# Tile sizes that shift where SBUF tiles lie, in a one-core hybrid encoder step

## The chip, the cores and the metric

The kernel runs on one core of one Trainium2 chip. The metric is device time of one execution in microseconds (us). Before the change the median of three runs is 1943.49 us (1939.63 to 1945.09).

## The reference, cut to what matters

One layer of a streaming encoder: 2048 prompt frames and 64 frames of a running stream, model width 1024. A combined input projection feeds three groups (a gated recurrence "HGRN2" with 8 heads, retention with 4 heads, cross-attention to 256 memory tokens with 4 heads); each group's output is multiplied by a SiLU gate, all three are concatenated to 2048 columns and go through one output projection, a residual and a final norm.

```python
def mixer_layer(x, pos, s_hg, s_rt, mem_k, mem_v, norm_g, w_in, lb, hg_norm_g, rt_norm_g, w_out):
    h = rms_norm(x, norm_g)
    proj = h @ w_in
    hg_q, hg_f, hg_i, hg_gate, rt_q, rt_k, rt_v, rt_gate, xa_q, xa_gate = jnp.split(proj, _split_points(), axis=-1)
    ...
    mixed = jnp.concatenate([o_hg, o_rt, o_xa], axis=-1)
    out = x + mixed @ w_out
    return out, s_hg_new, s_rt_new
```

All inputs and outputs are float32.

## The kernel before, in words

**Split products.** TensorE multiplies in a reduced form of float32 (`float32r`, F32R in the code). So that the products keep their accuracy, `split` (lines 239 to 241) turns every operand of a large product into a high part, which ScalarE rounds (line 240), and a low part, which VectorE gets as the difference (line 241). Each product is then three matmuls into the same accumulator: high with high, high with low, low with high. In `T.matmul(out, a, b)` the operand `a` is stationary (loaded into the array by LDWEIGHTS) and `b` is moving (streamed past it).

**Stages.** A short start makes the memory keys and values. Then two groups of tokens (0 to 1023, and 1024 to 2111 with the sample frames at the end) go through the input projections and the three head groups. Last comes the output stage from line 1192 on, one tile of 128 tokens after another, 16 of them and one of the 64 sample frames.

**The large products.**
- Line 249, in `gemm_col`: weights stationary, normed activations moving, 24 matmuls for each column tile of 128 outputs and up to 512 tokens. Tiles: `whi`, `wlo` from the pool `wpool`; `ha`, `hb` from `hpool`.
- Line 294, in `gemm_tok`: the same two families of tiles with their roles exchanged, activations stationary, 512 columns of weights moving.
- Lines 741 and 785, in the attention's tail: both operands are tiles `s` of the pool `wk`, which hold a split of queries, keys, values and softmax weights.
- Line 1180, in `y_half`: the output projection. Stationary are the split mixed activations `m`, tiles `s` of the pool `wk` that line 1042 takes and line 1048 fills; moving are the split output weights, which stand in `whi`/`wlo`, in the former places of `ha` and `hb`, and in two pairs of tiles `v` of `vpool` (the list `worder`, line 847). A half tile is 16 blocks of the contraction with three matmuls each, 48 in all; two halves make a token tile. For the 64 sample frames each half is 32 matmuls.

The smaller products are plain float32 and show up in the trace as two MATMUL records each: lines 516 to 581 for HGRN2 (line 563 with stationary `abuf`, line 566 with stationary `s` and moving state `Sn` or `Sc`), 620 to 693 for retention (moving `q2b` in line 637 and `r2` in line 653), 763 for attention.

**Order.** TensorE's and SyncE's order is that in which the code is written: `poll` (line 107) lets the tails of heads in between the large products when a modelled clock has passed their due times. The other engines are ordered by a scheduler. Tiles come from pools with a fixed number of buffers; `small` (line 223) takes little tiles for sums and scales from the pool `sm`, two buffers for those of 32 columns and three for the others. A tile that gets a buffer again waits for the readers of the buffer's former tile.

**Addresses.** Pools lie one behind the other in each SBUF partition, in the order of lines 74 to 87 (`const`, `wk`, `sm`, `vpool`, `qep`, `stt_p`, `hpool`, `wpool`, `stp`), and tiles inside a pool likewise, each rounded up to 32 bytes. Sizes of the large tiles, and the steps at which the matmuls cut them, are multiples of 256 bytes, so that everything in such a pool has one remainder modulo 256.

Of the kernel before, what the change touches and what calls it, by code (L numbers as in the profile page):

```python
# [7 lines left out]
F32 = mybir.dt.float32  # L8
# [7 lines left out]
P = 128  # L16
# [47 lines left out]
def layer_kernel(ctx: ExitStack, tc: tile.TileContext, io: dict):  # L64
    nc = tc.nc
    V, S, G, T = nc.vector, nc.scalar, nc.gpsimd, nc.tensor
    dma = nc.sync.dma_start
# [6 lines left out]
    const = ctx.enter_context(tc.tile_pool(name="const", bufs=1))  # L74
    wk = ctx.enter_context(tc.tile_pool(name="wk", bufs=16))
    sm = ctx.enter_context(tc.tile_pool(name="sm", bufs=3))
# [114 lines left out]
        wpos["credit"] += 1  # L191
        w_pump()

    cols = const.tile([P, 44], F32, name="cols")
    dma(cols, io["cols"])
    cst = const.tile([P, 396], F32, name="cst")
    ident = cst[:, 0:128]
    qdec = cst[:, 128:384].rearrange("p (a b) -> p a b", a=2)
# [2 lines left out]
    mask = const.tile([P, 512], U8, name="mask")  # L201
    ones = const.tile([P, P], F32, name="ones")
    G.memset(ones, 1.0)
    nhalf = const.tile([P, 4], F32, name="nhalf")
    G.memset(nhalf, -0.5)
    a_buf = []
    for i in range(2):
# [13 lines left out]
        return wk.tile([P, 512], dt, tag="s", name="s")  # L221

    def small(n, tag):
        return sm.tile([P, n], F32, tag=tag, name=tag, bufs=2 if n == 32 else 3)

    def acc():
        return p_acc.tile([P, 512], F32, tag="acc", name="acc")
# [77 lines left out]
    def stats_g(chunks, c0, gap):  # L305
        for i, src in enumerate(chunks):
            L = src.shape[0]
            ss = small(2, "ss2")
            for j in range(2):
                x = slot()  # L310
                dma(x[0:L], src[:, j * 512:(j + 1) * 512])
                S.activation(x[0:L], x[0:L], AF.Square, accum_out=ss[0:L, j:j + 1])
            rs = rsall[0:L, c0 + i:c0 + i + 1]
            G.tensor_tensor(out=rs, in0=ss[0:L, 0:1], in1=ss[0:L, 1:2], op=ALU.add)
            rsqrt_small(rs, rs, 1, 1.0 / D, EPS)
            rsdone.add(c0 + i)
            yield gap
# [113 lines left out]
    def hgrn_gemm(h, wf, wq, wg, ht, tok0, nt, vt, rel):  # L431
# [22 lines left out]
        for w in (1, 2, 4, 8):  # L454
# [3 lines left out]
            v4 = Gt[:, 0:ntp].rearrange("p (n t w) -> p n t w", t=2, w=w)  # L458
            V.tensor_tensor(out=v4[:, :, 0, :], in0=v4[:, :, 0, :], in1=bc(v4[:, :, 1, 0:1], [P, n, w]), op=ALU.mult)
        Te = small(32, "Te")[:, 0:nb].rearrange("p (c a) -> p c a", a=8)  # L460
        V.tensor_copy(Te, F[:, 0:ntp].rearrange("p (c a w) -> p c a w", a=8, w=SUB)[:, :, :, SUB - 1])
        rT = small(32, "rT")[:, 0:nb].rearrange("p (c a) -> p c a", a=8)
        V.reciprocal(out=rT, in_=Te)
        M = sm.tile([P, 4, 36], F32, tag="M", name="M", bufs=2)[:, 0:nch, :]
# [353 lines left out]
        hmap[gi, i] = ht  # L818
        hdone[gi, i] = done

    rsall = const.tile([P, 20], F32, name="rsall")
    t0 = const.tile([P, 8], F32, name="t0")
    V.tensor_tensor(out=t0, in0=cols[:, 0:8], in1=cols[:, 8:16], op=ALU.subtract)
    S.activation(t0, t0, AF.Tanh, scale=0.5)
    ca = const.tile([P, 8], F32, name="ca")
    cb = const.tile([P, 8], F32, name="cb")
    cnb = const.tile([P, 8], F32, name="cnb")
    hgg = const.tile([P, 12], F32, name="hgg")
    V.tensor_scalar(out=ca, in0=t0, scalar1=0.25, scalar2=0.75, op0=ALU.mult, op1=ALU.add)
    V.tensor_scalar(out=cb, in0=t0, scalar1=-0.25, scalar2=0.25, op0=ALU.mult, op1=ALU.add)  # L830
    V.tensor_scalar(out=cnb, in0=t0, scalar1=0.25, scalar2=-0.25, op0=ALU.mult, op1=ALU.add)
# [475 lines left out]
```

## Time and profile before

| | |
|---|---|
| median of 3 runs | 1943.49 us |
| the profiled execution | 1944.17 us, of which the trace's span is 1942.4 us |
| TensorE (PE) matmul busy | 1908.9 us, 98% |
| VectorE (DVE), ScalarE (ACT), GpSimd (POOL) busy | 54%, 30%, 7% |
| granted TensorE clock | 0.995 of full speed on average |
| memory read and written | 117.69 and 33.69 MB |

In a view by line, a row has line, engine, operation, output tile, input tiles (buffer numbers left out; of a MATMUL the moving one stands first), shape, count, busy time and mean duration. A view of one tile gives minimum, median and maximum duration in ns. A matmul's duration contains its way through the array, so that following matmuls overlap; how fast they follow is read from their starts, or from the chain of waits, where a piece gives start, length and the number of instructions in it.

### The profile page before, as it was taken

The numbers are of one execution on the slowest core, as the hardware profiler recorded it, in microseconds if no ns is written. First come the engines' busy times: TensorE is split into PE (matmuls) and PEld (weight loads), VectorE is DVE, ScalarE is ACT, GpSimd is POOL, SyncE is SP. The second block draws the span as 40 slices with busy tenths as digits, with TensorE's granted clock in tenths as the row PEclk, the third lists the DMA queues.
The fourth block names the chain that finished last, engine by engine and source line by source line (L and its number), as shares of the span: only waits on it lengthen the run. The fifth ranks groups of instructions, "written<-read, shape, count | busy, mean of one in ns | idle before, by whom it ended". The sixth has DMA issues, their size and how long they took to land.

```text
span 1942.4 us, 28116 instructions
## 1 busy us (share of the span) xinstructions
PE 1908.9 (98%) x10938; PEld 1618.5 (83%) x10938; DVE 1043.3 (54%) x2512; ACT 585.9 (30%) x1414; POOL 139.9 (7%) x335
## 2 busy tenths in 40 slices
PE   8999999999999999999999999999999999999998
PEld 7888788888888787988789998899989878888886
DVE  8527457753677557417637774477765642222222
ACT  7413232322333434312323332233333431111111
POOL 0001000000100100000101111021100000000000
PEclk9999999999999999999999999999999999999999
DMA  7512222111111424212211111111122342233322
GB/s 254 179 58 55 75 66 61 44 50 44 44 55 55 153 71 134 92 55 58 87 47 49 49 49 49 44 49 49 60 71 78 118 144 87 87 102 113 89 71 60
DMA packets 116742, 153.21 MB, mean 79 GB/s; under 512 B 13312, under 2 KB 79232, under 8 KB 116608
## 3 DMA queue, kind: packets, MB, share of 16 engines
q1 hardware_dynamic: 116608, 151.41, 25.4%
q8 instruction: 86, 1.41, 0.3%
q14 instruction: 48, 0.39, 0.1%
HBM read 117.69 MB, written 33.69 MB: 78 GB/s over the span
## 4 chain that ended last, share of the span: by engine, by line
PE 87%; DVE 6%; DMA 2%; ACT 2%; issue 1%; POOL 1%; SPq 0%; DVEq 0%; POOLq 0%; ACTq 0%
PE acc L249 39%; PE acc L1180 19%; PE acc L294 15%; PE scb L522 2%; PE ob L531 2%; PE ob L563 1%; PE ob L566 1%; PE acc L785 1%; PE ob L741 1%; PE acc L264 1%; PE tr L516 1%; PE tr L581 1%; PE tr L763 1%; DVE wlo L241 1%; ACT s L682 1%
## 5 line engine op out<-in xcount | busy, mean ns | idle before, releaser
L249 PE MATMUL acc<-hb,whi 128*128 128x320 f32 (+2 forms) x1696 | 409.1, 331 | 0.4 <-DVE hb L371 0.4
L249 PE MATMUL acc<-ha,whi 128*128 128x512 f32 x1120 | 354.7, 398 | 0.0
L249 PEld LDWEIGHTS acc<-hb,whi 128*128 128x128 f32 x1696 | 284.6, 189 | 25.0 <-issue 4.4
L241 DVE TENSOR_TENSOR wlo<-wst,whi 128x1024 fp32r<-128x1024 f32 x115 | 140.0, 1226 | 261.2 <-ACT whi L240 260.2
L249 PE MATMUL acc<-hb,wlo 128*128 128x256 f32 (+2 forms) x848 | 276.9, 327 | 0.0
L249 PEld LDWEIGHTS acc<-ha,whi 128*128 128x128 f32 x1120 | 205.0, 189 | 41.3 <-issue 2.6
L249 PE MATMUL acc<-ha,wlo 128*128 128x512 f32 x560 | 220.0, 393 | 0.0
L240 ACT CAST whi<-wst 128x1024 fp32r<-128x1024 f32 x115 | 119.7, 1051 | 211.4 <-PE acc L249 172.0
L249 PEld LDWEIGHTS acc<-hb,wlo 128*128 128x128 f32 x848 | 160.2, 189 | 11.2
L294 PE MATMUL acc<-whi,ha 128*128 128x512 f32 x512 | 161.0, 396 | 0.0
L294 PE MATMUL acc<-whi,hb 128*128 128x512 f32 x512 | 160.0, 394 | 0.0
L1180 PE MATMUL acc<-whi,s 128*128 128x512 f32 x396 | 125.9, 396 | 1.3 <-ACT s L240 1.0
L249 PEld LDWEIGHTS acc<-ha,wlo 128*128 128x128 f32 x560 | 105.7, 189 | 23.1 <-DVE wlo L241 0.2
L294 PEld LDWEIGHTS acc<-whi,hb 128*128 128x128 f32 x512 | 94.5, 188 | 19.8 <-issue 1.2
L294 PEld LDWEIGHTS acc<-whi,ha 128*128 128x128 f32 x512 | 93.8, 188 | 19.6 <-issue 1.3
L294 PE MATMUL acc<-wlo,ha 128*128 128x512 f32 x256 | 100.1, 391 | 0.0
L294 PE MATMUL acc<-wlo,hb 128*128 128x512 f32 x256 | 99.8, 390 | 0.0
L1180 PE MATMUL acc<-hb,s 128*128 128x512 f32 x400 | 97.7, 400 | 0.0
L1180 PE MATMUL acc<-ha,s 128*128 128x512 f32 x400 | 96.3, 396 | 0.0
L1180 PEld LDWEIGHTS acc<-hb,s 128*128 128x128 f32 x400 | 76.3, 191 | 18.4
L241 DVE TENSOR_TENSOR s<-mst,s 128x512 fp32r<-128x512 f32 (+1 forms) x64 | 40.4, 671 | 94.2 <-ACT s L240 94.2
L1180 PEld LDWEIGHTS acc<-whi,s 128*128 128x128 f32 x396 | 74.3, 188 | 19.6 <-ACT s L240 1.3
(236 smaller groups left out, 2913.3 us busy)
## 6 DMA issues: line engine op xcount, KB each, us to landing
wst<-w_in_t SPq DMA_DIRECT2D x104, 512.0 KB, 4.0
mixT<-s SPq DMA_DIRECT2D x64, 256.0 KB, 4.3
mst<-mixT SPq DMA_DIRECT2D x30, 512.0 KB, 5.9
wst<-w_out_t SPq DMA_DIRECT2D x16, 512.0 KB, 4.0
xq<-x_prompt SPq DMA_DIRECT2D x18, 256.0 KB, 5.0
o_yp<-xq SPq DMA_DIRECT2D x18, 256.0 KB, 2.3
s<-mixT SPq DMA_DIRECT2D x16, 256.0 KB, 3.0
s<-x_prompt SPq DMA_DIRECT2D x16, 256.0 KB, 5.3
```

The lines of the kernel that those rows point to most:

```text
L240: S.copy(hi, src)
L241: V.tensor_tensor(out=lo, in0=src, in1=hi.bitcast(F32), op=ALU.subtract)
L249: T.matmul(ps[:, 0:nt], w[a][:, kk, :], ht[b][:, kk, 0:nt], start=(n == 0), stop=(n == 23))
L264: T.matmul(ps[:, 0:nt], w[a][:, kk, :], ht[b][:, kk, 0:nt], start=(kk == 0 and a + b == 0), stop=(kk == KT - 1 and a == 1))
L294: T.matmul(ps[0:L, :], ht[b][:, kk, o:o + L], w[a][:, kk % 2, :], start=(n == 0), stop=(n == 23))
L516: T.transpose(trk[:, c * 128:(c + 1) * 128], kch[:, c * 128:(c + 1) * 128], ident)
L522: T.matmul(scb[32 * e:32 * e + 32, c * 128 + 32 * e:(c + 1) * 128], K[:, c * 128 + 32 * e:c * 128 + 32 * e + 32], Qe[:, c, E_OFF[e]:E_OFF[ ...
L531: T.matmul(db[:, c * 128:(c + 1) * 128], kT[:, c * 128:(c + 1) * 128], vt[c], start=True, stop=True)
L563: T.matmul(ob[:, c * 128:(c + 1) * 128], A[:, c * 128:(c + 1) * 128], vt[c], start=True, stop=first)
L566: T.matmul(ob[:, c * 128:(c + 1) * 128], qst[:, c * 128:(c + 1) * 128], st[c][0], start=False, stop=True)
L581: T.transpose(tro[:, c * 128:(c + 1) * 128], on[:, c * 128:(c + 1) * 128], ident)
L1180: T.matmul(ps, m[a][:, kk % 4], w[b], start=(n == 0), stop=(n == 16 * len(terms) - 1))
```

## The change

No instruction is added, removed or moved on any engine: apart from names and line numbers each engine's row of instructions is the same (`nhalf` is set over 16 columns instead of 4). What differs is sizes:

```diff
-    cols = const.tile([P, 44], F32, name="cols")
-    dma(cols, io["cols"])
+    cols = const.tile([P, 60], F32, name="cols")
+    dma(cols[:, 0:44], io["cols"])
...
-    nhalf = const.tile([P, 4], F32, name="nhalf")
+    nhalf = const.tile([P, 16], F32, name="nhalf")
...
     def small(n, tag):
-        return sm.tile([P, n], F32, tag=tag, name=tag, bufs=2 if n == 32 else 3)
+        return sm.tile([P, n], F32, tag=tag, name=tag, bufs=2 if n == 32 or tag in ("rs1", "mu", "rc", "rs4", "nm", "sum", "ss2") else 3)
...
-    rsall = const.tile([P, 20], F32, name="rsall")
+    rsall = const.tile([P, 64], F32, name="rsall")
+    hgg = rsall[:, 20:32]
...
-    hgg = const.tile([P, 12], F32, name="hgg")
```

The tile `hgg` (halved gains of the heads) becomes a part of `rsall` (the tokens' norm factors, columns 0 to 18). Seven kinds of little tiles have two buffers instead of three. From this the tiles' addresses follow, as the two programs place them, as remainders modulo 256 bytes:

| tiles | before | after |
|---|---|---|
| `s` (`wk`): stationary in line 1180, both operands in 741 and 785 | 192 | 128 |
| `v` (`vpool`), `Qe`, `Sn`/`Sc`, `ha`/`hb`, `whi`/`wlo`, the staging tiles | 160 | 128 |
| `abuf`, `r2`, `q2b`, `sp` (`const`) | 160 | 0 |
| `cst` with the identity | 64 | 128 |
| `ones` | 128 | 192 |

So in lines 249 and 294 both operands have one remainder before and after, in lines 741 and 785 too; in line 1180 the stationary operand's was 192 and the moving one's 160, and now both are 128. In line 563 both were 160, and now they are 0 and 128; in lines 637 and 653 they were 160 and 192, and now 0 and 128.

## The prediction

> **What bounds the kernel now.** I read the page first, then the chain of waits in order of time, then the tiles of the large products.
>
> ```profile
> span 1942.4 us, 28116 instructions
> ...
> PE 1908.9 (98%) x10938; PEld 1618.5 (83%) x10938; DVE 1043.3 (54%) x2512; ACT 585.9 (30%) x1414; POOL 139.9 (7%) x335
> ...
> PEclk9999999999999999999999999999999999999999
> ...
> PE 87%; DVE 6%; DMA 2%; ACT 2%; issue 1%; POOL 1%; SPq 0%; DVEq 0%; POOLq 0%; ACTq 0%
> PE acc L249 39%; PE acc L1180 19%; PE acc L294 15%; PE scb L522 2%; PE ob L531 2%; PE ob L563 1%; PE ob L566 1%; PE acc L785 1%; PE ob L741 1%; PE acc L264 1%; PE tr L516 1%; PE tr L581 1%; PE tr L763 1%; DVE wlo L241 1%; ACT s L682 1%
> ```
>
> TensorE is busy for 98% of the span and carries 87% of the chain, at a clock that stays in the highest digit throughout. So the kernel's time is a number of matmuls multiplied by the distance at which one follows the other. An edit that only moves tiles can act here through that distance. The chain in order of time gives it (start, length, what, count):
>
> ```profile
> 83.75 55.76 PE acc L294 x246
> ...
> 253.03 19.73 PE acc L249 x87
> 306.11 6.85 PE acc L249 x30
> 327.11 7.53 PE acc L249 x33
> ...
> 1572.85 362.34 PE acc L1180 x1546
> ```
>
> In the long pieces the 512-column matmul costs 55.76 / 246 = 226.7 ns in line 294 and 19.73 / 87 = 226.8 ns in line 249. In line 1180 it is 362.34 / 1546 = 234.4 ns. That last number contains the waits of the output stage's first tile, so I take the cadence of whole token tiles from VectorE, which adds the residual right behind each half (the timeline of VectorE; `xq` and `abuf` alternate by tile):
>
> ```profile
> 1708.39 1.29 DVE L241 TENSOR_TENSOR s<-mst,s 128x512 fp32r<-128x512 f32 x2 [0.51 <-ACT s L240]
> ...
> 1718.68 0.69 DVE L1189 TENSOR_TENSOR xq<-xq,acc 128x512 f32<-128x512 f32 x1 [8.39 <-PE acc L1180]
> ...
> 1741.08 0.69 DVE L1189 TENSOR_TENSOR abuf<-abuf,acc 128x512 f32<-128x512 f32 x1 [8.32 <-PE acc L1180]
> ```
>
> From 1718.68 to 1741.08 us are 22.40 us for one tile of 96 matmuls: 233.3 ns each, 6.5 ns more than the same shape costs in lines 249 and 294. The views of lines 294 and 1180 show the same difference with one and the same moving tile:
>
> ```profile
> L294 PE MATMUL acc<-whi,ha x512: 387/389/504, 83.6 to 1207.9; 128*128 128x512 f32 x171
> ...
> L1180 PE MATMUL acc<-whi,s x396: 392/396/500, 1552.0 to 1931.7; 128*128 128x512 f32 x198
> ```
>
> The moving `whi` (named first) goes past a stationary `ha` in line 294 and the matmul takes 389 ns; in line 1180 it goes past a stationary `s` and it takes 396 ns (minimum, median, maximum; these durations overlap). The shape, the moving tile and the order of the three terms are the same in both lines; the stationary tile is not. Line 1180 pairs a stationary `s` at remainder 192 modulo 256 with a moving tile at 160. Line 294 pairs 160 with 160. Is it that 192 is a bad place for a stationary tile? The attention's second product has both operands at 192:
>
> ```profile
> L785 PE MATMUL acc<-s x144: 192/387/397, 662.6 to 1572.5; 128*128 128x512 f32 x72, 128*128 128x256 f32 x48, 128*128 128x64 f32 x24
> ```
>
> Its median, which falls to the 512-column matmuls (half of all, and the longest), is 387 ns. So what goes with the slow matmuls is the difference between the two operands' remainders, not either remainder.
>
> **The change part by part.** *Line 1180: 192 against 160 becomes 128 against 128.* I take it that the matmul then costs what it costs with equal remainders elsewhere. For the chain's last piece that is 1546 x (233.3 - 226.8 ns) = 10.0 us. It lies wholly on the path: the piece runs to 7 us before the end, and nothing else is on it. What is late next? The following tile's operands would be the candidate. Their last split (line 241, 1708.39 + 1.29 = 1709.68 us) is done 9.0 us before the matmuls that need it, which begin about when the tile before ends (1718.68 us). A tile gets shorter by 96 x 6.5 ns = 0.6 us, so this cover holds.
>
> *Lines 249 and 294: equal remainders, 160 before, 128 after.* I take 0. Two places with equal remainders, 160 and 192, cost the same within 2 ns in the medians above, so a third one should. There is something to gain here, though. Shorter pieces, which start behind the tail of a head, cost more per matmul:
>
> ```profile
> 145.51 2.77 PE acc L294 x12
> ...
> 321.86 4.82 PE acc L249 x21
> ```
>
> They are 2.77 - 12 x 0.2268 = 0.05 us and 4.82 - 21 x 0.2268 = 0.06 us above the long pieces' rate; the 30 and 33 above are 0.05 us over as well. Each seems to pay once for its start. If part of that is the switch between tiles of different remainders, some of it goes. With 40 HGRN2 tails and 20 of attention (8 and 4 heads on 5 token tiles) and 17 of retention, at three or four stages each, there are some 240 such starts, worth 12 us in all. I take 0 and let half of it, 6 us, set the range's lower end.
>
> *The plain float32 products with `const` tiles: lines 563, 637 and 653 now pair 128 with 0.* The timeline of TensorE in the HGRN2 tail, and the groups by shape:
>
> ```profile
> 1163.86 0.39 PE L563 MATMUL ob<-v,abuf 128*128 128x128 f32 x2
> 1164.08 0.39 PE L566 MATMUL ob<-Sc,s 128*128 128x128 f32 x2
> 1164.30 0.39 PE L563 MATMUL ob<-v,abuf 128*128 128x128 f32 x2
> 1164.53 0.39 PE L566 MATMUL ob<-Sn,s 128*128 128x128 f32 x2
> ```
>
> ```profile
> L563 PE MATMUL ob<-v,abuf 128*128 128x128 f32 x272 | 51.1, 274 | 0.0
> ...
> L653 PE MATMUL ob<-r,s 128*128 128x256 f32 x60 | 17.9, 380 | 0.0
> L637 PE MATMUL scb<-q2b,s 128*128 128x256 f32 x64 | 17.7, 401 | 2.9 <-ACT s L628 2.8
> ```
>
> Line 563 has both operands at 160, line 566 has 160 and 192, and each takes 0.22 us per pair of records. These products do not care about a difference of 32. The nearest price for a difference of 128, should they care about that, is line 1180's: (272 + 60 + 64) x 6.5 ns = 2.6 us. The other end is a like gain, since lines 637 and 653 differ by 32 already: 124 x 6.5 ns = 0.8 us. I take 0, by the row nearest to it.
>
> *Two buffers instead of three for seven kinds of little tiles.* A writer now waits for the reader two uses back instead of three. In the view of TensorE's waits stands what hangs on them today:
>
> ```profile
> PE ob L741 <- DVE s L574: 4.3, 2, 2.2
> ...
> PE tr L693 <- DVE s L685: 1.4, 2, 0.8
> ```
>
> Lines 574 and 685 read `rs`; TensorE waits for them 5.7 us in all. What would queue behind such a wait is GpSimd's next pair of lines 236 and 237 and then VectorE's line 574. The readers of two tails back are several hundred matmuls in the past, so I take 0; the upper bound is that these waits double, 5.7 us. A gain is excluded, because a buffer less can release nothing earlier. `nhalf`, `cols` and `hgg` inside `rsall` cost 0: they are written at the start, and `hgg` is read in columns that nobody writes later.
>
> The sum is -10.0 us. Against the profiled execution, 1944.17 - 10.0 = 1934.2 us. The median of the runs shown is 0.7 us below that execution, so the time should be 1943.49 - 10.0 = 1933.5 us.
>
> **The rivals.** *The address has nothing to do with it.* Line 1180 could be slower for another reason that goes with the output stage: 48 matmuls into one accumulator instead of 24, or stores and loads beside it. Then nothing changes: 1943.5 us. For it speaks that no matmul of the output stage has equal remainders, so the trace has no counterexample inside the stage. Against it speaks that line 1180 is slow on every one of its moving tiles while the other engines do less there than in the projections. The Trainium skill (SBUF — State Buffer, section "Who interferes with whom") gives TensorE two separate read ports in SBUF, one for the moving operand and one for LDWEIGHTS, and says that "PE and ACT never wait on anyone". By that rule no placement could matter and the result would be this one; the 389 against 396 ns with one moving tile disagree with it as far as a trace of one kernel can. I give it 15%.
>
> *Half of it.* The difference modulo 256 may be one condition of several, such as which part of the memory the two tiles lie in. If line 1180 settles halfway, at 230 ns, the gain is 1546 x 3.3 ns = 5.1 us: 1938.4 us, 0.26% and so within what can be told. 7%.
>
> *Slower: 128 is a bad shared place.* Both good pairs of the trace lie at odd multiples of 32 or 64 (160 and 192). None lies at 128. If tiles at 128 get in each other's way as 192 and 160 do, line 1180 gains nothing and the projections pay:
>
> ```profile
> L249 PE MATMUL acc<-ha,whi 128*128 128x512 f32 x1120 | 354.7, 398 | 0.0
> L249 PE MATMUL acc<-ha,wlo 128*128 128x512 f32 x560 | 220.0, 393 | 0.0
> L249 PE MATMUL acc<-hb,whi 128*128 128x512 f32 x544 | 171.8, 397 | 0.0
> L294 PE MATMUL acc<-whi,ha 128*128 128x512 f32 x512 | 161.0, 396 | 0.0
> L294 PE MATMUL acc<-whi,hb 128*128 128x512 f32 x512 | 160.0, 394 | 0.0
> ...
> L249 PE MATMUL acc<-hb,wlo 128*128 128x512 f32 x272 | 106.5, 391 | 0.0
> L294 PE MATMUL acc<-wlo,ha 128*128 128x512 f32 x256 | 100.1, 391 | 0.0
> L294 PE MATMUL acc<-wlo,hb 128*128 128x512 f32 x256 | 99.8, 390 | 0.0
> ```
>
> These are 4032 matmuls of 512 columns; at 6.5 ns each they cost 26.2 us, which makes 1969.7 us. It decides the sign once they lose 10.0 us / 4032 = 2.5 ns each while line 1180 still gains. Against it speaks that 160 and 192, two different places, cost the same. 8%.
>
> **How the numbers follow.** The forecast has 70%, the rivals 15, 7 and 8. What a measurement of this kernel can tell from no change is about 0.3%, 5.8 us. Faster by more than that is the forecast alone; within it are the first two rivals, 22%; slower is the last, 8%. The forecast's own bounds are 1933.5 - 0.8 - 6 = 1926.7 and, with 2.6 us of float32 products and 5.7 us of waits, 1941.8 us. To reach eight in ten, the range must take in part of the other cases: 1927.0 to 1943.5 us holds the forecast's cases, the half and half of the case without change, and leaves out some 16%.
>
> **What the changed profile would show.** If each step is right: a token tile in the output stage takes 96 x 226.8 ns = 21.8 us instead of 22.4, the last piece of the chain has about 226.8 ns per matmul, and the median of line 1180's MATMUL rows falls from 396 to about 389 ns. Line 249's and 294's long pieces stay at 226.7 to 226.8 ns, line 563's pairs at 0.22 us, and TensorE's waits behind lines 574 and 685 at about 6 us. The prediction is wrong if line 1180 stays at 233 ns, or if it falls and lines 249 and 294 give it back.

## The result, and the profile after

The changed kernel takes 1930.89 us (median of 6 runs, 1929.27 to 1935.75); the kernel before, with the runs made beside it, 1941.96 us (6 runs, 1939.63 to 1947.36). The ratio is 0.9943 with a 95% interval of 0.9924 to 0.9963: 0.4 to 0.8% faster, about 11 us. The forecast was 1933.5 us, in a range of 1927.0 to 1943.5.

The profiled execution's span went from 1942.4 to 1932.0 us, 10.4 us less. Its page and its chain of waits in order of time:

```profile
span 1932.0 us, 28118 instructions
...
PE 1899.2 (98%) x10938; PEld 1620.5 (84%) x10938; DVE 1043.5 (54%) x2512; ACT 585.9 (30%) x1414; POOL 141.3 (7%) x335
```

```profile
83.77 55.77 PE acc L294 x246
...
252.96 19.72 PE acc L249 x87
306.01 6.85 PE acc L249 x30
326.96 7.53 PE acc L249 x33
...
1572.06 352.75 PE acc L1180 x1546
```

TensorE is busy for 9.7 us less with the same number of matmuls. The page counts two instructions more than before: they are one semaphore instruction each on ScalarE and on GpSimd, so the rows of those two engines are not quite the same, though the section on the change says so. The kernel of run b below has both of them too and takes as long as the kernel before. The projections' pieces shown are the same to 0.01 us, and the output stage's begins 0.8 us earlier and is 9.6 us shorter. VectorE's residual additions show the cadence of its token tiles, and the view of lines 1180 and 294 the matmuls' durations (minimum, median, maximum):

```profile
1704.34 1.29 DVE L241 TENSOR_TENSOR s<-mst,s 128x512 fp32r<-128x512 f32 x2 [0.39 <-ACT s L240]
...
1714.48 0.69 DVE L1189 TENSOR_TENSOR xq<-xq,acc 128x512 f32<-128x512 f32 x1 [8.26 <-PE acc L1180]
...
1736.24 0.69 DVE L1189 TENSOR_TENSOR abuf<-abuf,acc 128x512 f32<-128x512 f32 x1 [7.55 <-PE acc L1180]
```

```profile
L1180 PE MATMUL acc<-whi,s x396: 388/389/500, 1549.9 to 1921.5; 128*128 128x512 f32 x198
```

```profile
L294 PE MATMUL acc<-whi,ha x512: 387/390/502, 83.6 to 1205.5; 128*128 128x512 f32 x171
```

A tile takes 21.76 us, 226.7 ns for each of its 96 matmuls, where it took 22.40 us. Line 1180's matmul now lasts what line 294's does. The float32 pairs and TensorE's waits behind the little tiles:

```profile
1161.41 0.38 PE L563 MATMUL ob<-v,abuf 128*128 128x128 f32 x2
1161.62 0.39 PE L566 MATMUL ob<-Sc,s 128*128 128x128 f32 x2
1161.85 0.39 PE L563 MATMUL ob<-v,abuf 128*128 128x128 f32 x2
```

```profile
PE ob L741 <- DVE s L574: 4.1, 2, 2.1
...
PE tr L693 <- DVE s L685: 1.4, 2, 0.8
```

Both are as before: 0.22 us a pair and 5.5 us of waits (5.7 before).

### The profile page after: what moved, and what is told of

Read it like the earlier page. It is cut to its first block, busy times and chain, and to the rows that moved or that the text cites. A ratio compares the mean times of both kernels' runs of the same rounds, so it can differ in the third digit from the quotient of the medians.

```text
span 1932.0 us, 28118 instructions
## 1 busy us (share of the span) xinstructions
PE 1899.2 (98%) x10938; PEld 1620.5 (84%) x10938; DVE 1043.5 (54%) x2512; ACT 585.9 (30%) x1414; POOL 141.3 (7%) x335
## 4 chain that ended last, share of the span: by engine, by line
PE 88%; DVE 6%; ACT 2%; DMA 2%; issue 1%; POOL 1%; SPq 0%; DVEq 0%; POOLq 0%; ACTq 0%
PE acc L249 39%; PE acc L1180 18%; PE acc L294 16%; PE scb L522 2%; PE ob L531 2%; PE ob L563 1%; PE ob L566 1%; PE acc L785 1%; PE ob L741 1%; PE acc L264 1%; ACT s L682 1%; PE tr L516 1%; PE tr L763 1%; PE tr L581 1%; POOL rs L237 1%
## 5 line engine op out<-in xcount | busy, mean ns | idle before, releaser
L294 PEld LDWEIGHTS acc<-whi,ha 128*128 128x128 f32 x512 | 93.9, 188 | 19.3 <-issue 1.3
```

Source lines behind the costliest of these rows:

```text
L294: T.matmul(ps[0:L, :], ht[b][:, kk, o:o + L], w[a][:, kk % 2, :], start=(n == 0), stop=(n == 23))
```

## The experiments

**The theories.** Theory 1: a 512-column matmul is slower when its two operands differ in their remainder modulo 256. Theory 2: something else in the change made the gain, namely the place 128 itself, the constants at 0, or the little tiles' buffers. The first two runs take one from the other.

### Only the difference removed (a_pad32_before)

```diff
 (kernel before)
+    sm.tile([P, 8], F32, tag="pad", name="pad", bufs=1)
```

> The kernel before with one unused tile of 32 bytes in the pool of little tiles, so that everything behind that pool moves by 32 bytes: both operands of line 1180 then lie at 192 modulo 256, constants and buffer counts are as before. Theory 1 (the difference of the two operands' remainders counts): a token tile of the output stage takes 21.8 us instead of 22.4 and the time falls by 9 to 11 us. Theory 2 (what helped is the place 128, or the constants at 0, or the little tiles' two buffers): the tile stays at 22.4 us and the time within 2 us of before.

### Only the difference put back (b_pad32_after)

```diff
 (changed kernel)
+    sm.tile([P, 8], F32, tag="pad", name="pad", bufs=1)
```

> The changed kernel with the same unused 32 bytes: the moving operands of line 1180 lie at 160 and the stationary at 128, all else is as changed. Theory 1: the token tile is back at 22.4 us and the time at that of the kernel before, within 2 us. Theory 2: 21.8 us and a gain of 9 to 11 us as in the changed kernel.

The inserted line moves every later line number by one. Chain and residual additions of the first of these two, then of the second:

```profile
1570.73 352.15 PE acc L1181 x1546
```

```profile
1690.80 0.69 DVE L1190 TENSOR_TENSOR abuf<-abuf,acc 128x512 f32<-128x512 f32 x1 [7.89 <-PE acc L1181]
...
1712.55 0.69 DVE L1190 TENSOR_TENSOR xq<-xq,acc 128x512 f32<-128x512 f32 x1 [8.04 <-PE acc L1181]
```

```profile
1570.24 360.82 PE acc L1181 x1546
```

```profile
1692.15 0.69 DVE L1190 TENSOR_TENSOR abuf<-abuf,acc 128x512 f32<-128x512 f32 x1 [8.77 <-PE acc L1181]
...
1714.55 0.69 DVE L1190 TENSOR_TENSOR xq<-xq,acc 128x512 f32<-128x512 f32 x1 [8.36 <-PE acc L1181]
```

With 32 unused bytes the kernel before has a tile cadence of 21.75 us and takes 1933.04 us (5 runs; ratio 0.9956, 0.9942 to 0.9969). That is 8.7 us less, a little under the 9 to 11 expected. With the same 32 bytes the changed kernel is back at 22.40 us a tile and takes 1941.15 us (ratio 0.9997, 0.9988 to 1.0005; the kernel before beside both 1941.75 us). So the gain is the difference of remainders, all of it within what these runs can tell: the tile's cadence and the last piece (352.15 us) are those of the changed kernel. The place 128, the constants at 0 and the buffers made no difference that can be measured, and theory 2 falls.

### Differences of 128 and of 64 bytes (c_diff128, d_diff64)

```diff
 (kernel before)
-        ... bufs=2 if n == 32 else 3)
+        ... bufs=2 if n == 32 or tag in ("rs1", "mu", "rc") else 3)     # c_diff128
+        ... bufs=2 if n == 32 or tag in ("rs1",) else 3)                # d_diff64
```

> The kernel before with two buffers instead of three for rs1, mu and rc alone: the stationary operand of line 1180 lies at 192, the moving at 64, a difference of 128. If the class is modulo 256 (theory 1): token tile 22.4 us. If modulo 128 or less would do: 21.8 us. The attention's products, both operands at 192, stay as they are.

> The kernel before with two buffers instead of three for rs1 alone: stationary at 192, moving at 128, a difference of 64. If the class is modulo 256 or 128: token tile 22.4 us. If modulo 64 would do: 21.8 us.

The residual additions with 128 bytes between the operands, then with 64:

```profile
1691.73 0.69 DVE L1189 TENSOR_TENSOR abuf<-abuf,acc 128x512 f32<-128x512 f32 x1 [8.73 <-PE acc L1180]
...
1714.04 0.69 DVE L1189 TENSOR_TENSOR xq<-xq,acc 128x512 f32<-128x512 f32 x1 [8.78 <-PE acc L1180]
```

```profile
1695.39 0.69 DVE L1189 TENSOR_TENSOR abuf<-abuf,acc 128x512 f32<-128x512 f32 x1 [8.90 <-PE acc L1180]
...
1717.79 0.69 DVE L1189 TENSOR_TENSOR xq<-xq,acc 128x512 f32<-128x512 f32 x1 [8.46 <-PE acc L1180]
```

22.31 and 22.40 us: a difference of 128 costs nearly as much as one of 32 (232.4 against 233.3 ns a matmul), and one of 64 as much. A class modulo 64 or 128 would not do. (One run each, 1938.65 and 1943.28 us, beside 1941.75 us of the kernel before. A single time decides nothing here; the reading rests on the cadence.)

### The distance measured by itself (p_probe)

```diff
 (changed kernel, behind the last store)
+    hi, lo = wt[n_in]          # two resident weight tiles, seen as 1024 columns
+    def probe(n, mo, so=0, plain=False):
+        ps = acc()
+        T.matmul(sep[:, 0:1], ones, ones[:, 0:1], start=True, stop=True)
+        for i in range(64):
+            st = lo[:, so + i % 2 * 128:so + i % 2 * 128 + 128]
+            mv = hi[:, mo:mo + n]
...
+            T.matmul(ps[:, 0:n], st, mv, start=True, stop=True)
+    for mo in (0, 4, 8, 16, 24, 32, 40, 48, 56, 64, 128):   # columns of 4 bytes
+        probe(512, mo)
+    probe(512, 8, 8)
+    for n in (320, 256):
+        for mo in (0, 8, 32):
+            probe(n, mo)
+    for mo in (0, 8, 32):
+        probe(128, mo, 0, True)
```

> The changed kernel with blocks of 64 matmuls appended behind its last store, one block for each distance between the moving and the stationary operand (two resident weight tiles, 512 columns: 0, 16, 32, 64, 96, 128, 160, 192, 224, 256 and 512 bytes; then both shifted by 32; then 320 and 256 columns and plain float32 of 128 columns at 0, 32 and 128 bytes); their products go nowhere. Theory 1 (class modulo 256): 64 x 226.8 ns = 14.5 us in the blocks at 0, 256, 512 and with both shifted, 64 x 233.3 ns = 14.9 us in the others. Rival (a smaller modulus): 14.5 us at 64 or 128 bytes too. Plain float32 should take the same at all three distances. If narrower products feel it like the wide ones, 320 and 256 columns are about 6 ns a matmul slower at 32 and 128 bytes than at 0.

Its timeline of TensorE (start, length; rows of the one-column separators left out). The first twelve rows are, in this order, 0, 16, 32, 64, 96, 128, 160, 192, 224, 256 and 512 bytes, and both shifted by 32; then come 320 columns, 256 columns and plain float32, each at 0, 32 and 128 bytes:

```profile
1919.00 14.80 PE L1221 MATMUL acc<-whi,wlo 128*128 128x512 f32 x64
...
1933.77 15.07 PE L1221 MATMUL acc<-whi,wlo 128*128 128x512 f32 x64
...
1948.82 15.17 PE L1221 MATMUL acc<-whi,wlo 128*128 128x512 f32 x64
...
1963.96 14.91 PE L1221 MATMUL acc<-whi,wlo 128*128 128x512 f32 x64
...
1978.85 15.18 PE L1221 MATMUL acc<-whi,wlo 128*128 128x512 f32 x64
...
1994.01 15.12 PE L1221 MATMUL acc<-whi,wlo 128*128 128x512 f32 x64
...
2009.10 15.23 PE L1221 MATMUL acc<-whi,wlo 128*128 128x512 f32 x64
...
2024.31 15.17 PE L1221 MATMUL acc<-whi,wlo 128*128 128x512 f32 x64
...
2039.45 15.17 PE L1221 MATMUL acc<-whi,wlo 128*128 128x512 f32 x64
...
2054.60 14.80 PE L1221 MATMUL acc<-whi,wlo 128*128 128x512 f32 x64
...
2069.38 14.80 PE L1221 MATMUL acc<-whi,wlo 128*128 128x512 f32 x64
...
2084.15 14.81 PE L1221 MATMUL acc<-whi,wlo 128*128 128x512 f32 x64
...
2098.93 9.64 PE L1221 MATMUL acc<-whi,wlo 128*128 128x320 f32 x64
...
2108.55 9.63 PE L1221 MATMUL acc<-whi,wlo 128*128 128x320 f32 x64
...
2118.16 9.63 PE L1221 MATMUL acc<-whi,wlo 128*128 128x320 f32 x64
...
2127.77 7.91 PE L1221 MATMUL acc<-whi,wlo 128*128 128x256 f32 x64
...
2135.65 7.72 PE L1221 MATMUL acc<-whi,wlo 128*128 128x256 f32 x64
...
2143.35 7.84 PE L1221 MATMUL acc<-whi,wlo 128*128 128x256 f32 x64
...
2151.17 14.54 PE L1221 MATMUL acc<-whi,wlo 128*128 128x128 f32 x128
...
2165.68 14.54 PE L1221 MATMUL acc<-whi,wlo 128*128 128x128 f32 x128
...
2180.20 14.54 PE L1221 MATMUL acc<-whi,wlo 128*128 128x128 f32 x128
```

At 0, 256 and 512 bytes, and with both operands shifted alike, a block takes 14.80 or 14.81 us. At every other distance that was tried it takes 14.91 (64 bytes) to 15.23 us, up to (15.23 - 14.80) / 64 = 6.7 ns more per matmul. (All blocks are some 0.3 us longer than expected: a row ends with the last matmul's way through the array, and the first matmuls of a block are slow.) It is a class modulo 256, and what counts is the distance and not the place. Two expectations failed in part. At 64 bytes the cost is 1.7 ns here, though the output stage paid all of it at that distance; so how much a wrong distance costs depends on something else too. The blocks differ from the output stage in the sequence of tiles and in that no block accumulates, and which of these it is was not tried. And narrower products do not follow: with 320 columns 0, 32 and 128 bytes cost the same (9.64, 9.63, 9.63), and with 256 columns the unequal operands are quicker, by 0.19 us in 64 (3 ns each) at 32 bytes and by 0.07 us at 128. Plain float32 takes 14.54 us at all three distances.

### The difference brought into the projections (g_wpad32)

```diff
 (kernel before)
+    wpool.tile([P, 8], F32, tag="pad", name="pad", bufs=1)
```

> The kernel before with the unused 32 bytes at the head of the pool of weight tiles: whi and wlo lie at 192, the activations ha and hb still at 160, s at 192. Theory 1 (difference modulo 256): the 4032 matmuls of 512 columns in the projections go from 226.8 to 233.3 ns, 26.2 us more; in the output stage the 600 matmuls that move whi or wlo past s now have equal remainders and get 6.5 ns faster, 3.9 us less, while those that move ha, hb or v stay at 233.3 ns; the 864 matmuls of 256 columns may get up to 3.3 ns faster by the blocks measured apart (2.9 us). In all 19 to 22 us slower than the kernel before. If the output stage's gain had been particular to that stage: projections as before, and a time within 5 us of before.

The chain in order of time, and the view of line 1180, here 1181 (249 and 294 are 250 and 295):

```profile
83.90 57.40 PE acc L295 x246
...
255.77 20.30 PE acc L250 x87
...
309.62 7.00 PE acc L250 x30
...
1589.17 358.29 PE acc L1181 x1546
```

```profile
L1181 PE MATMUL acc<-ha,s x400: 395/396/500, 1578.2 to 1935.9; 128*128 128x512 f32 x134
...
L1181 PE MATMUL acc<-whi,s x396: 389/392/499, 1568.9 to 1944.0; 128*128 128x512 f32 x198
L1181 PE MATMUL acc<-wlo,s x204: 389/389/398, 1570.0 to 1944.2; 128*128 128x512 f32 x102
```

The projections take on the cost: 57.40 / 246 and 20.30 / 87 are 233.3 ns in both lines. And inside the output stage the two kinds now stand side by side: `wlo`, which shares the remainder of `s`, at a median of 389 ns, and `ha`, which does not, at 396. That settles the rival "the address has nothing to do with it" within one stage. `whi` shares the remainder too and lies between, at 392: its first matmuls behind a run of `ha` still follow each other at 230 to 236 ns.

The kernel is slower, 1956.49 us against 1942.56 (ratio 1.0076, 1.0062 to 1.0089), but by 14 us and not by 19 to 22; the two profiled spans differ by 12.2 us. The two traces have the same 10938 MATMUL records in the same order, so the change of each distance from one start to the next can be summed by line. The 512-column matmuls of lines 249 and 294 take 21.1 us longer, where 26.2 were expected. Of that, 1.8 us are not the addresses: they fall into stretches in which one of the two traces shows a granted clock of 0.5, or are waits. The other 3988 of the 4032 matmuls cost 19.3 us more, 4.8 ns each. The price expected, 6.5 ns, is nearly paid by the matmuls from the twelfth of a piece on (6.3 ns), but only half of it by the first eleven (3.1 ns), because a piece starts at a slow pace in the kernel before already: one of 30 went from 6.85 to 7.00 us, 5 ns a matmul. Line 1180 is 4.2 us shorter; 1.5 us of this are such a stretch of low clock, which the kernel before has at the start of the stage and this one has not, so that 2.6 us are left of the 3.9 expected. The products of 256 columns in line 249 gave 1.3 of the 2.9 us that were possible. Changes of over 100 ns at single places outside those stretches, waits among them, come to 4.2 us less in all; one pair of traces can't tell these from scatter.

### The constants in the same class too (e_const128, h_const128_again)

```diff
 (changed kernel)
-    nhalf = const.tile([P, 16], F32, name="nhalf")
+    nhalf = const.tile([P, 48], F32, name="nhalf")
...
-    rsall = const.tile([P, 64], F32, name="rsall")
+    rsall = const.tile([P, 32], F32, name="rsall")
```

> The changed kernel with 48 columns for nhalf and 32 for rsall: abuf, r2 and q2b lie at 128 like all pools, instead of at 0. If a difference between float32 operands costs nothing (the prediction's term of 0): the same time as the changed kernel within 1 us, token tile 21.8 us. If it costs as in line 1180 (2.6 us): 1 to 3 us faster than the changed kernel, and line 563's pairs shorter than 0.22 us.

Beside it ran the changed kernel:

> The changed kernel unaltered on the same chip, so that the one with moved constants has its neighbour: 9 to 11 us faster than the kernel before, token tile 21.8 us.

The first pair gave 1930.14 us (ratio to before 0.9934, 0.9921 to 0.9946) and 1933.26 us for the changed kernel (0.9947, 0.9933 to 0.9960). Line 563's pairs stayed at 0.22 us and the last piece of the chain was the same:

```profile
1568.82 352.06 PE acc L1180 x1546
```

```profile
1572.13 352.15 PE acc L1180 x1546
```

The 3 us lay ahead of the output stage. About half of them shows in the traces as clock: from 749.9 to 753.4 us the changed kernel's has a granted clock of 0.51, with matmuls of line 249 at 427 ns, and the other's 1.00 (1.6 us). The rest is changes of over 150 ns at single places, waits among them. Nothing of this points to the constants, so both ran again:

> The kernel with the constants at 128 once more, beside the changed kernel: if the 3 us between their medians were due to the constants, again 2 to 4 us faster than the changed kernel; if they are the scatter of the waits ahead of the output stage, within 1.5 us on either side.

> The changed kernel once more, neighbour of the one with the constants at 128: 9 to 11 us faster than the kernel before.

This time it was 1933.83 us (0.9950, 0.9937 to 0.9962) with the constants moved and 1932.73 us (0.9951, 0.9938 to 0.9965) without. The order of the two is reversed. The constants' place has no effect that these runs can tell, and no version tried is clearly faster than the changed kernel.

## Why the prediction was right, point by point

- **The bound.** That a change of the distance between matmuls passes wholly into the time held: TensorE is 9.7 us less busy, the span is 10.4 us shorter.
- **Line 1180, 10.0 us.** The matmul was put at 226.8 ns and came to 226.7; the last piece became 9.6 us shorter here (362.34 to 352.75) and 10.2 us in the changed kernel's second profile (352.15). One reading beside it was wrong. That 362.34 us make 234.4 ns a matmul and not 233.3 was put down to waits of the stage's first tile, and the clock was read as full throughout from a row of 40 slices, which is too coarse to show a few microseconds: from 1572.7 to 1576.0 us the granted clock is 0.50, eight matmuls there take up to 574 ns from start to start, six of them 426 or 427, and this makes the 1.5 us. The trace after, and the second one, have such a stretch at the same place, so the difference of the pieces holds to within the 0.6 us by which those two differ. The tile's 0.6 us of lost cover did no harm: the next tile's last split is done at 1704.34 + 1.29 = 1705.63 us, 8.9 us before the tile ends (1714.48 us). The cause was read rightly from two pairs of rows, and the runs a and b show it. The forecast of 1933.5 us lies 2.6 us above the measured 1930.89; 1.5 us of this is that the kernel before, too, came out lower beside it than in its first three runs.
- **Lines 249 and 294, 0.** Long pieces are the same to 0.01 us; the short ones moved by up to 0.05 us, some down and some up (a piece of 21 in line 249 from 4.82 to 4.77 us, the next from 4.78 to 4.81). The 6 us that the lower end of the range held ready for the starts of pieces did not come. The guess was that part of a piece's slow start is a switch between remainders. The 22 pieces of line 249 behind line 531 speak against it: line 531's tiles lay at 160 and 192 before, and after the change at 128 like the piece's own, and yet these pieces lie above 226.7 ns a matmul by 105 ns on average before and by 112 ns after. In the blocks with equal operands, too, 64 matmuls take 1933.63 - 1919.00 = 14.63 us from the first start to the separator behind, 0.12 us more than 64 x 226.7 ns. Of this, 0.09 us is the first matmul behind the separator (314 ns); then the next ten or so follow at 224 to 236 ns, and the rest at a steady 227.
- **Float32 products with constants, 0.** Right: 0.22 us a pair before and after, and equal blocks at 0, 32 and 128 bytes.
- **Little tiles, 0.** Right: TensorE's waits behind them are 5.5 us against 5.7, and run b, which has two buffers, equals the kernel before.
- **The rivals.** "Nothing changes" and "half of it" fell with the result, in which line 1180 went all the way to 226.7 ns; that it is the address, and nothing else of the output stage, is shown by runs a, b and g. "128 is a bad shared place" fell with the result: 128 works as 160 and 192 do. Its price, 26.2 us for the projections, was too high: run g paid 19.3 us of it, because the price counted every matmul from the long pieces' pace.
- **The rule of two separate read ports** (the Trainium skill, SBUF — State Buffer, section "Who interferes with whom"), by which TensorE waits on nobody, does not foretell this case: the distance between the addresses of its two operands is worth up to 6.7 ns per 512-column matmul. That its two reads wait for each other is not shown by that.
- **What was not seen.** About 0.8 us of the profile's 10.4 us lies ahead of the output stage. In the other profiles with equal remainders in line 1180 that stage's piece starts between 1568.82 and 1572.13 us, against 1572.85 before; since it starts at 1570.24 us in run b, which has no gain, I take this for scatter and not for an effect. Part of the scatter is the clock: every trace has some stretches of about 3.4 us at half the granted clock, and whether large products run in them differs from run to run (before from 648 and from 1573 us on, after from 24 and from 1570 us on, for example).

## What to carry to other kernels

When one shape of matmul has two paces in one trace, compare the addresses of the two operands before looking for a wait: here 32 bytes of padding were worth what the whole change was. Put tiles that meet in wide float32r matmuls at equal remainders modulo 256, and look at the pools in the order in which they lie, since a few bytes of scalars move everything behind them. The cost shows most in long runs of 512-column matmuls. At the distances tried (32 and 128 bytes), products of 320 columns and plain float32 of 128 columns paid nothing, and those of 256 columns went slightly the other way. Before a few microseconds between two traces are explained, compare their granted clocks in windows of a few microseconds.

## What the runs showed of the hardware that was not expected

- The pace has a run-in. After a break, matmuls with equal remainders too begin at 224 to 236 ns and settle at 226.7 after some ten. In run g this also happens without a break, where `whi` with equal remainders follows a run of `ha` with unequal ones. With unequal remainders they do not settle: in run g they stay at 231 to 235 ns. A piece of 30 matmuls therefore feels a difference less (6.85 against 7.00 us, 5 ns each) than one of 246 (55.76 against 57.40 us, 6.7 ns each).
- The distance to the next instruction's stationary operand seems to count as well, across kinds. From the last 512-column matmul of a piece in line 249 to line 563 (stationary `abuf`) the median distance of starts in 23 cases was 229 ns with both at 160, 233 ns with 128 and 0, and in run e, with both at 128, 228 ns again. To line 531 (stationary `s`, 22 cases) it was 233 to 234 ns with 160 and 192 and 228 ns with both at 128. It is no full rule: to line 531 it was 226 to 234 ns in run a with both at 192, and 226 to 230 ns in run d with 64 bytes between them.
- Between stretches of full clock, every trace shows a few of about 3.4 us, some of twice that, at a granted clock of 0.5, in which 512-column matmuls follow each other at 427 ns. A page's row of 40 slices and its mean of 0.995 hide them.
- Why the memory or the array behaves so was not shown. The runs show a period of 256 bytes and a dependence on the distance; what repeats every 256 bytes stays open.
